# Two-layer hybrid decoder: the spatial-gating constants prepared during branch C's value projection, and the final norm's last squares summed on TensorE

## The chip, the cores and the metric

The kernel runs on one core of a Trainium2 chip. The time is that of one execution on the device in microseconds (us); lower is better. PE is TensorE's matmul row in the profile, PEld its weight loads, DVE is VectorE, ACT ScalarE, POOL GpSimd, SP SyncE; PEq, ACTq and SPq are the queues of these engines, from which DMAs are issued.

## The reference

Two layers on x of 512 tokens by 1024 channels, all float32, then a final RMSNorm. For each layer:

```
h = rmsnorm(x);  proj = h @ w_in
A: differential attention      C: mixture of dilated window attentions
B: vb = layernorm(gelu(..)) in chunks of 128 tokens
   mixed = einsum('gts,bnsgc->bntgc', sgu_w * tril, vb) + sgu_b
   yb = u * mixed * silu(bz)
merged = sum over branches of sigmoid(gate) * (y_branch @ w_branch)
x = x + merged @ w_out
```

What the change touches is B's `mixed`, whose constants are the masked `sgu_w` and a bias, and the final `rmsnorm`, which needs the sum of the squares of 1024 channels for each token.

## The kernel before

Channels lie on the partitions, in eight blocks of 128 (KC = 8), tokens along the free axis. Every large product is made of three float32r matmuls (L408 to L411): a weight tile is split into a rounded part `whi` (ACT, L170) and a remainder `wlo` (DVE, every fifth on POOL, L171). The weights come from HBM in tiles `raw` of 512 KB through SP's queue (L151). Two such tiles have buffers, so a load starts when the tile two places earlier has been split. Six split slots lie ahead of TensorE. Some units ("S") are Strassen products: their operands are first combined by POOL and DVE (L192 to L195), and seven products of 256 columns (`seven`, L503) are added on DVE and POOL (L528) through the tiles `ea`, `eb` and `zs`.

The order of a layer is the list in `plan()`: B's and A's value projections, C's value projection ("val C", during which `mix` on ACT and DVE prepares the Strassen operands of h), attention A with projections as filling, attention C with projections as filling, then the first gate group, `("sgu",)`, the other gate groups between the branch projections `pb`, and the output projection `out`. Within this program order a scheduler places the instructions of each engine by their readiness and priority. At run time each engine runs its own instructions strictly in order.

`i_sgu` (L657) runs right after attention C. On ACT's queue it issues the load of the bias row, broadcast to all partitions, and of the 128x512 weights (L661, L662). `behind_weights` orders these behind the newest weight split. POOL masks the weights (L666). TensorE sums their columns with a matmul by ones (L671) into `ps_s`, of which there is one buffer. DVE makes `add` of that, the bias and a layernorm parameter in four instructions (L675). Then come, for each of four groups, four matmuls (L685), two DVE instructions (L690, L695), and a split into `yB` (L414, L415). `add` lies in a buffer of the tag "t1", which `seven` uses for `eb`.

In the last layer the output blocks 4 to 7 are made in two halves of 256 tokens, LT and RT. For each block `square` (L278) takes squares on ACT (L284) and adds them to `ss` on POOL (LT) or DVE (RT), L288; block 7's stay apart. `final` (L824) has TensorE sum `ss` and block 7's squares over the channels (L386, a matmul for each tile and 128 tokens, each in two passes), DVE scales (L391), POOL takes the power -0.5 (L393), DVE and TensorE spread the result (L400, L405), and eight DVE multiplications and stores follow (L829, L830).

Of the kernel before, what the change touches and what calls it, by code (L numbers as in the profile page):

```python
# [10 lines left out]
F32 = mybir.dt.float32  # L11
# [4 lines left out]
ALU = mybir.AluOpType  # L16
# [3 lines left out]
P = 128  # L20
D = 1024
# [79 lines left out]
def hybrid_kernel(ctx: ExitStack, tc, xT, posr, wpack, tabs, cvec, pvec, rvec, lamv, sguw, outT):  # L101
# [149 lines left out]
    class X:  # L251


        def __init__(self, first=False):
            self.first = first
            self.h = att.tile([P, KC, S], F32R, tag="vs", name="xuh")
            self.l = []
            self.f = []
            self.ss = t2k("ob", name="ssum")

        def raw(self, kc):
            if kc % 2 == 0:
# [15 lines left out]
        def square(self, kc, c=slice(0, S), part=False):  # L278
            xf = self.f[kc // 2][:, kc % 2, c]
            if kc == 0:  # L280
                A.activation(out=self.ss[:, c], in_=xf, func=AF.Square)
            else:
                sq = t2k("t1", name="sq")
                A.activation(out=sq[:, c], in_=xf, func=AF.Square)  # L284
                if part and kc == KC - 1:
                    self.sq = sq
                    return
                (V if kc == KC - 1 or self.first or c.start else G).tensor_tensor(out=self.ss[:, c], in0=self.ss[:, c], in1=sq[:, c], op=ALU.add)  # L288

# [90 lines left out]
    def rms_sum(sqs):  # L380

        n = sqs[0].shape[-1] // P
        ps = ps_s()[:, 0, :]
        for b in range(n):
            for i, sq in enumerate(sqs):
                T.matmul(  # L386
                    ps[:, b : b + 1], lhsT=sq[:, b * P : (b + 1) * P], rhs=ones[:, 0:1], start=i == 0,
                    stop=i == len(sqs) - 1,
                )
        ro = sm.tile([P, 4], F32, tag="ro", name="ro")[:, :n]  # L390
        V.tensor_scalar(out=ro, in0=ps[:, :n], scalar1=1.0 / D, scalar2=EPS, op0=ALU.mult, op1=ALU.add)  # L391
        rp = sm.tile([P, 4], F32, tag="rp", bufs=2, name="rp")[:, :n]
        G.tensor_tensor(out=rp, in0=ro, in1=mhalf[:, :n], op=ALU.pow)  # L393
        return rp
# [153 lines left out]
    def layer(l, xu, parts):  # L548
# [47 lines left out]
        def mix(kc):  # L596
            with behind_weights():
                if kc == 0:
                    split_x(KC - 1)
                    norm["mix"] = mixes(xu.f)  # L600
                next(norm["mix"])
                if kc == KC - 1:
                    next(norm["mix"])
                    if l == 0:
                        lambdas()

        def pair(it, use, bank=ps_pj):

# [47 lines left out]

        def i_sgu():  # L657
            vb, uz = sgu["vb"], sgu["uz"]
            sgw = [att.tile([P, S], F32, tag="kl", bufs=2, name="sgw") for _ in range(2)]
            with behind_weights():  # L660
                nc.scalar.dma_start(out=sgw[0], in_=rvec[l : l + 1, :].partition_broadcast(P))  # L661
                nc.scalar.dma_start(out=sgw[1], in_=sguw[l])  # L662
            t = att.tile([P, 2, 4, S], F32R, tag="vs", name="yB")
            yhl[BR_B] = [[t[:, 0, 0:2], t[:, 0, 2:4]], [t[:, 1, 0:2], t[:, 1, 2:4]]]
            wc = sgw[1].rearrange("p (g t) -> p g t", g=4)
            G.affine_select(  # L666
                out=wc, in_=wc, pattern=[[0, 4], [1, P]], base=0, channel_multiplier=-1, compare_op=ALU.is_ge,
                fill=0.0,
            )
            pw = ps_s()[:, 0, :]  # L670
            T.matmul(pw, lhsT=ones, rhs=sgw[1], start=True, stop=True)  # L671
            add = t2k("t1", name="add")
            for g in range(4):
                gs = slice(g * P, (g + 1) * P)
                V.scalar_tensor_tensor(  # L675
                    out=add[:, gs], in0=pw[:, gs], scalar=ln[:, l, 1, g : g + 1], in1=sgw[0][:, gs], op0=ALU.mult,
                    op1=ALU.add,
                )
            yield 0.9
            for g in range(4):  # L680
                if g % 2 == 0:
                    pms = ps_s()
# [1 line left out]
                for tb in range(4):  # L684
                    T.matmul(  # L685
                        pm[:, tb * P : (tb + 1) * P], lhsT=vb[:, tb, g * P : (g + 1) * P],
                        rhs=wc[:, g, :], start=True, stop=True,
                    )
                ob = t2k("ob")
                V.scalar_tensor_tensor(  # L690
# [6 lines left out]
                )  # L697
                split(yhl[BR_B][0][g // 2][:, g % 2, :], yhl[BR_B][1][g // 2][:, g % 2, :], ob)
                yield 0.9

        def i_val(br):
            if br == BR_A:
# [12 lines left out]
            for tb in range(4):  # L715
# [4 lines left out]
                    out=o[:, :, 64:128], in0=p8, scalar=r, in1=o[:, :, 0:64].bitcast(F32), op0=ALU.mult,  # L720
                    op1=ALU.subtract,
                )

        def i_pp(br, i):
            def use(n, ps, own):
# [97 lines left out]

        def final(c):  # L824
            x_ = xn[0]
            bc = rms_spread(rms_sum([x_.ss[:, c], x_.sq[:, c]]))
            for e in range(KC):
                xf = x_.f[e // 2][:, e % 2, c]
                V.scalar_tensor_tensor(out=xf, in0=xf, scalar=fg[:, e : e + 1], in1=bc, op0=ALU.mult, op1=ALU.mult)  # L829
                (nc.sync, nc.scalar)[e % 2].dma_start(out=outT[e, :, c], in_=xf)  # L830
# [317 lines left out]
```

## Time and profile before

| what | us |
|---|---|
| median of 3 runs | 1116.62 (1115.82 to 1116.85) |
| the profiled execution | 1117.34 |
| its span, first to last instruction | 1115.6 |
| PE busy | 1087.3 (97%) |
| DVE busy | 823.6 (74%) |
| ACT busy | 598.9 (54%) |
| POOL busy | 471.4 (42%) |

Shares are averages over the whole span. Where PE is idle in a stretch, the wait that ended last there tells what it stood for; idle time of the other engines costs nothing by itself.

### The profile page before, as it was taken

Reading aid. Unit: us, or ns where it says so; the run is one execution under the profiler, and the core shown is the slowest. Engines: PE = TensorE matmul, PEld = TensorE weight load, DVE = VectorE, ACT = ScalarE, POOL = GpSimd, SP = SyncE. Lnnn points to the kernel's source line nnn. Section 1 sums busy time; section 2 is a strip of 40 time slices with the busy share of each in tenths; the row PEclk is TensorE's granted clock in tenths of the full one; section 3 lists DMA queues with packets and bytes.
Section 4 is the critical chain, followed back from the end, with each engine's and each line's share of the span. In section 5 each row is a group of like instructions: output and inputs, shape, how many; then the busy total and the mean of one; then the engine's idle time right before and its main releaser. Section 6 shows DMA issues by size and latency. Waiting matters only on the chain.

```text
span 1115.6 us, 17803 instructions
## 1 busy us (share of the span) xinstructions
PE 1087.3 (97%) x6444; PEld 939.6 (84%) x6444; DVE 823.6 (74%) x1519; ACT 598.9 (54%) x1281; POOL 471.4 (42%) x419
## 2 busy tenths in 40 slices
PE   8999999999999999999999999999999999999996
PEld 6787878878778999998888888887888889999886
DVE  6678869877969877774436779787788877787544
ACT  6554747486774444453435456565778534444430
POOL 4004443434534676644211343534342536667420
PEclk9999999999999999999999999999999999999998
DMA  5431313220312233244523313122111313333433
GB/s 194 135 103 58 95 58 96 95 76 1 114 58 87 87 112 102 92 148 152 188 83 103 98 38 114 57 76 76 58 58 57 112 59 101 107 97 103 142 110 99
DMA packets 35064, 105.97 MB, mean 95 GB/s; under 512 B 4704, under 2 KB 7776, under 8 KB 34976
## 3 DMA queue, kind: packets, MB, share of 16 engines
q1 hardware_dynamic: 29936, 98.50, 27.6%
q10 hardware_dynamic: 5040, 6.34, 1.8%
q8 instruction: 51, 0.84, 0.3%
q14 instruction: 37, 0.30, 0.1%
HBM read 100.58 MB, written 4.24 MB: 94 GB/s over the span
## 4 chain that ended last, share of the span: by engine, by line
PE 85%; DVE 5%; DMA 3%; issue 2%; ACT 2%; POOL 1%; POOLq 0%; DVEq 0%; SPq 0%; ACTq 0%
PE ps_pj L409 15%; PE ps_pj L411 14%; PE ps_pj L410 14%; PE ps_to L409 8%; PE ps_to L411 8%; PE ps_to L410 8%; PE ps_s L858 3%; DMA raw<-in_wpack 2%; PE ps_to L898 2%; PE ps_to L434 2%; PE ps_to L436 2%; PE ps_to L435 2%; DVE wlo L171 1%; PE ps_to L929 1%; PE ps_to L1004 1%
## 5 line engine op out<-in xcount | busy, mean ns | idle before, releaser
L170 ACT ACTIVATE whi<-raw 128x512 fp32r<-128x512 f32 x316 | 195.0, 627 | 246.3 <-DMA raw<-in_wpack 74.2
L171 DVE TENSOR_TENSOR wlo<-raw,whi 128x512 fp32r<-128x512 f32 x261 | 223.0, 862 | 99.2 <-ACT whi L170 91.1
L409 PE MATMUL ps_pj<-xh,whi 128*128 128x512 f32 (+1 forms) x544 | 207.9, 382 | 1.0 <-DVE z L462 1.0
L411 PE MATMUL ps_pj<-xh,wlo 128*128 128x512 f32 (+1 forms) x544 | 204.5, 376 | 0.0
L410 PE MATMUL ps_pj<-xl,whi 128*128 128x512 f32 (+1 forms) x544 | 204.0, 375 | 0.0
L171 POOL TENSOR_TENSOR wlo<-raw,whi 128x512 fp32r<-128x512 f32 x55 | 78.8, 1433 | 169.6 <-ACT whi L170 158.2
L409 PEld LDWEIGHTS ps_pj<-xh,whi 128*128 128x128 f32 x544 | 102.6, 189 | 20.0 <-issue 1.6
L411 PEld LDWEIGHTS ps_pj<-xh,wlo 128*128 128x128 f32 x544 | 102.5, 188 | 18.2 <-issue 0.9
L410 PEld LDWEIGHTS ps_pj<-xl,whi 128*128 128x128 f32 x544 | 102.7, 189 | 17.6 <-issue 1.8
L452 POOL TENSOR_TENSOR rsh<-rsh,sinr 128x512 f32<-128x512 f32 x32 | 42.3, 1322 | 132.8 <-DVE rsh L450 121.3
L171 DVE TENSOR_TENSOR wlo<-t,whi 128x512 fp32r<-128x512 f32 x88 | 81.2, 940 | 16.2 <-ACT whi L170 16.0
L411 PE MATMUL ps_to<-mh,wlo 128*128 128x256 f32 x320 | 90.5, 284 | 0.5 <-DVE wlo L171 0.4
L409 PE MATMUL ps_to<-mh,whi 128*128 128x256 f32 x320 | 90.8, 284 | 0.2 <-ACT ea L531 0.2
L410 PE MATMUL ps_to<-ml,whi 128*128 128x256 f32 x320 | 90.4, 283 | 0.0
L874 ACT ACTIVATE pr<-pr,nm 128x128 f32<-128x128 f32 (+3 forms) x128 | 70.6, 553 | 36.4 <-DVE nm L870 36.1
L170 ACT ACTIVATE whi<-t 128x512 fp32r<-128x512 f32 x112 | 65.8, 624 | 42.0 <-DVE t L193 23.4
L409 PE MATMUL ps_to<-xh,whi 128*128 128x256 f32 x240 | 68.5, 285 | 2.6 <-DVE zs L528 2.5
L411 PE MATMUL ps_to<-xh,wlo 128*128 128x256 f32 x240 | 68.4, 286 | 0.7 <-DVE wlo L171 0.7
L410 PE MATMUL ps_to<-xl,whi 128*128 128x256 f32 x240 | 68.2, 284 | 0.0
L870 DVE CUSTOM_DVE_ANT_0 pr<-ps_s,tab 128x128 f32<-128x128 f32 (+3 forms) x128 | 56.2, 483 | 11.8 <-PE ps_s L858 8.3
L409 PEld LDWEIGHTS ps_to<-mh,whi 128*128 128x128 f32 x320 | 61.4, 192 | 1.0 <-ACT ea L531 0.4
L411 PEld LDWEIGHTS ps_to<-mh,wlo 128*128 128x128 f32 x320 | 61.3, 192 | 1.2 <-DVE wlo L171 0.9
(238 smaller groups left out, 2844.9 us busy)
## 6 DMA issues: line engine op xcount, KB each, us to landing
raw<-in_wpack SPq DMA_DIRECT2D x174, 512.0 KB
xf<-in_xT SPq DMA_DIRECT2D x8, 256.0 KB
xr<-in_xT ACTq DMA_DIRECT2D x8, 256.0 KB
x1d<-xf SPq DMA_DIRECT2D x8, 256.0 KB
raw<-in_wpack SPq DMA_DIRECT2D x4, 256.0 KB
xr<-x1d ACTq DMA_DIRECT2D x4, 256.0 KB
xr<-x1d ACTq DMA_DIRECT2D x8, 128.0 KB
out<-xf SPq DMA_DIRECT2D x8, 128.0 KB
```

What stands on the lines that cost most here:

```text
L170: newest[0] = A.activation(out=hi, in_=src, func=AF.Copy).ins
L171: r = (G if on_g else V).tensor_tensor(out=lo, in0=src, in1=hi.bitcast(F32), op=ALU.subtract)
L409: T.matmul(ps, lhsT=wh, rhs=mh, start=first, stop=False)
L410: T.matmul(ps, lhsT=wh, rhs=ml, start=False, stop=False)
L411: T.matmul(ps, lhsT=wl, rhs=mh, start=False, stop=last)
L434: T.matmul(banks[tb], lhsT=mh_[:, ts], rhs=wh, start=kc == 0, stop=False)
L435: T.matmul(banks[tb], lhsT=ml_[:, ts], rhs=wh, start=False, stop=False)
L436: T.matmul(banks[tb], lhsT=mh_[:, ts], rhs=wl, start=False, stop=kc == KC - 1)
L452: G.tensor_tensor(out=sh, in0=sh, in1=sinr, op=ALU.mult)
L858: T.matmul(pss[:, m, at[i]], lhsT=q[HALF[m], a, qs], rhs=k[HALF[m], b, :W], start=t == 0, stop=t == 2,)
L870: V.tensor_tensor_reduce(out=o, in0=pss[:, m, at[i]], in1=tab[:, 0 if br == BR_A else 1, S - W :], op0=ALU.add, op1=ALU.min, scale=-0.125, ...
L874: A.activation(out=o, in_=o, func=AF.Exp, scale=-1.0, bias=nm[:, m : m + 1], accum_out=den[:, m : m + 1],)
```

## The change

The loads of the gating constants and the mask on POOL move into `gating()`, which is called in val C at its third block (kc = 2). The column sum on TensorE and the four DVE instructions move into `gating_add()`, called at the end of val C; they write over the bias tile and no longer take a "t1" buffer. `i_sgu` keeps its four groups only. In the final norm, block 6's squares are no longer added to `ss`: TensorE sums three tiles. For the halves it takes `ss` first for both 128-token groups, then block 6, then block 7, into two banks, and DVE's scaling is done for each group.

```diff
@@ square
-                if part and kc == KC - 1:
-                    self.sq = sq
+                if part and kc >= KC - 2:
+                    self.sq[kc] = sq
                     return
@@ rms_sum
-        ps = ps_s()[:, 0, :]
-        for b in range(n):
-            for i, sq in enumerate(sqs):
-                T.matmul(
-                    ps[:, b : b + 1], lhsT=sq[:, b * P : (b + 1) * P], rhs=ones[:, 0:1], start=i == 0,
-                    stop=i == len(sqs) - 1,
-                )
+        ps2 = ps_s()
+        todo = [(b, i) for b in range(n) for i in range(len(sqs))]
+        if n == 2:
+            todo.sort(key=lambda t: t[1])
+        sums = [ps2[:, b % 2 if n == 2 else 0, b : b + 1] for b in range(n)]
+        for b, i in todo:
+            T.matmul(
+                sums[b], lhsT=sqs[i][:, b * P : (b + 1) * P], rhs=ones[:, 0:1], start=i == 0, stop=i == len(sqs) - 1
+            )
...
-        V.tensor_scalar(out=ro, in0=ps[:, :n], scalar1=1.0 / D, scalar2=EPS, op0=ALU.mult, op1=ALU.add)
+        for o, p in [(ro, ps2[:, 0, :n])] if n == 4 else [(ro[:, b : b + 1], sums[b]) for b in range(n)]:
+            V.tensor_scalar(out=o, in0=p, scalar1=1.0 / D, scalar2=EPS, op0=ALU.mult, op1=ALU.add)
@@ mix
+                if kc == 2:
+                    gating()
@@ i_sgu
-            sgw = [att.tile([P, S], F32, tag="kl", bufs=2, name="sgw") for _ in range(2)]
-            with behind_weights():
-                nc.scalar.dma_start(out=sgw[0], in_=rvec[l : l + 1, :].partition_broadcast(P))
-                nc.scalar.dma_start(out=sgw[1], in_=sguw[l])
...
-            G.affine_select(
...
-            pw = ps_s()[:, 0, :]
-            T.matmul(pw, lhsT=ones, rhs=sgw[1], start=True, stop=True)
-            add = t2k("t1", name="add")
-            for g in range(4):
-                gs = slice(g * P, (g + 1) * P)
-                V.scalar_tensor_tensor(
-                    out=add[:, gs], in0=pw[:, gs], scalar=ln[:, l, 1, g : g + 1], in1=sgw[0][:, gs], op0=ALU.mult,
-                    op1=ALU.add,
-                )
-            yield 0.9
+            add, wc = sgu["w"]
@@ new
+        def gating():
+
+            sgu["w"] = add, wc = [att.tile([P, S], F32, tag="kl", bufs=2, name="sgw") for _ in range(2)]
+            with behind_weights():
+                nc.scalar.dma_start(out=add, in_=rvec[l : l + 1, :].partition_broadcast(P))
+                nc.scalar.dma_start(out=wc, in_=sguw[l])
+            w4 = wc.rearrange("p (g t) -> p g t", g=4)
+            G.affine_select(
+                out=w4, in_=w4, pattern=[[0, 4], [1, P]], base=0, channel_multiplier=-1, compare_op=ALU.is_ge,
+                fill=0.0,
+            )
+
+        def gating_add():
+            add, wc = sgu["w"]
+            pw = ps_s()[:, 0, :]
+            T.matmul(pw, lhsT=ones, rhs=wc, start=True, stop=True)
+            for g in range(4):
+                gs = slice(g * P, (g + 1) * P)
+                V.scalar_tensor_tensor(
+                    out=add[:, gs], in0=pw[:, gs], scalar=ln[:, l, 1, g : g + 1], in1=add[:, gs], op0=ALU.mult,
+                    op1=ALU.add,
+                )
@@ final
-            bc = rms_spread(rms_sum([x_.ss[:, c], x_.sq[:, c]]))
+            bc = rms_spread(rms_sum([x_.ss[:, c], x_.sq[KC - 2][:, c], x_.sq[KC - 1][:, c]]))
```

The first place is DVE's queue at the end of attention C in layer 0. Before (`y` are the splits of A's output, `ob` at L1013 the joining of C's two halves, `ea` and `eb` the sums of a Strassen product):

```order
L415 TENSOR_TENSOR ptl<-ps_to,pth 128x4x128 x2
L415 TENSOR_TENSOR y<-yf,y 128x512 x2
L528 TENSOR_TENSOR ea<-ps_pj,ea 128x256
L1013 TENSOR_TENSOR ob<-ps_to,ob 64x512
L171 TENSOR_TENSOR wlo<-t_3399,whi 128x512
L171 TENSOR_TENSOR wlo<-t_3398,whi 128x512
L171 TENSOR_TENSOR wlo<-t_3399,whi 128x512
L1013 TENSOR_TENSOR ob<-ps_to,ob 64x512
L415 TENSOR_TENSOR y<-yf,y 128x512
L171 TENSOR_TENSOR wlo<-raw,whi 128x512
L1014 SCALAR_TENSOR_TENSOR yf<-ob,zs 128x512
L675 SCALAR_TENSOR_TENSOR add<-ps_s,pv,sgw 128x128 x4
```

The same place with the change, where the lines of the file have moved by 4 to 12 (L678 is the former L690, L683 the former L695):

```order
L419 TENSOR_TENSOR ptl<-ps_to,pth 128x4x128 x2
L532 TENSOR_TENSOR ea<-ps_pj,ea 128x256
L171 TENSOR_TENSOR wlo<-t_3410,whi 128x512
L171 TENSOR_TENSOR wlo<-t_3409,whi 128x512
L678 SCALAR_TENSOR_TENSOR ob<-ps_s,pv,sgw 128x512
L171 TENSOR_TENSOR wlo<-t_3410,whi 128x512
L419 TENSOR_TENSOR y<-yf,y 128x512 x2
L683 SCALAR_TENSOR_TENSOR ob<-ob,uz 128x512
L1025 TENSOR_TENSOR ob<-ps_to,ob 64x512
L532 TENSOR_TENSOR eb<-ps_pj,ea 128x256
L419 TENSOR_TENSOR y<-yf,y 128x512
L1025 TENSOR_TENSOR ob<-ps_to,ob 64x512
```

The four `add` instructions are gone from here, the first gating group stands ahead of the splits of `y`, and so do `ea` and the weight splits.

The second place is DVE's queue at the end of val C in layer 0, with the change (`vs` are C's values, `ml` and `tm` the Strassen operands):

```order
L500 TENSOR_TENSOR tm<-xf,tm 128x512
L368 TENSOR_SCALAR sg<-pv 128x1 x2
L707 SCALAR_TENSOR_TENSOR sgw<-ps_s,pv,sgw 128x128 x2
L419 TENSOR_TENSOR ml<-tm,mh 128x512
L707 SCALAR_TENSOR_TENSOR sgw<-ps_s,pv,sgw 128x128 x2
L730 SCALAR_TENSOR_TENSOR vs<-ps_to,rp,vs 128x8x64 x2
```

The four instructions of L707 are new in this place; what stands around them is as before, except that it comes after them.

The third place is the end of TensorE's queue. Before, and then with the change:

```order
L411 MATMUL ps_to<-mgh,xl 128x256
L386 MATMUL ps_s<-ones,ssum 128x1
L386 MATMUL ps_s<-ones,sq 128x1
L386 MATMUL ps_s<-ones,ssum 128x1
L386 MATMUL ps_s<-ones,sq 128x1
L405 MATMUL ps_s<-dg,ones 128x256
```

```order
L414 MATMUL ps_to<-mgl,xh 128x256
L415 MATMUL ps_to<-mgh,xl 128x256
L390 MATMUL ps_s<-ones,ssum 128x1 x2
L390 MATMUL ps_s<-ones,sq 128x1 x4
L409 MATMUL ps_s<-dg,ones 128x256
```

Two matmuls more, and only the last two of them read block 7's squares. The same six stand, for LT, in one piece ahead of the second RT block; the four of before stood around that block's first three matmuls.

## Rows read from the trace of the kernel before

**Rows 1.** The page's first part: busy time, share of the span, instructions

```profile
PE 1087.3 (97%) x6444; PEld 939.6 (84%) x6444; DVE 823.6 (74%) x1519; ACT 598.9 (54%) x1281; POOL 471.4 (42%) x419
```

**Rows 2.** Windows: length, busy time of each engine, PE clock, DMA share, GB/s

```profile
325.00:365.00 40.00, 36.02 (x247) 31.64 (x246) 38.31 (x56) 20.94 (x38) 21.26 (x16) 1.00 0.38 118
870.00:915.00 45.00, 40.07 (x272) 36.15 (x271) 38.51 (x60) 23.48 (x43) 19.32 (x15) 0.96 0.34 106
0.00:8.00 8.00, 2.84 (x7) 2.27 (x8) 3.10 (x10) 5.02 (x9) 1.63 (x8) 1.00 0.71 229
1104.90:1115.63 10.73, 2.27 (x11) 1.47 (x10) 4.57 (x12) 0.42 (x1) 0.70 (x1) 0.65 0.36 121
```

**Rows 3.** Waits of PE, 320 to 365 us: waiter, releaser, total us, times, longest

```profile
PE ps_s L685 <- DVE add L675: 1.3, 1, 1.3
PE ps_pj L409 <- DVE ea L528: 0.7, 1, 0.7
...
PE ps_s L671 <- POOL sgw L666: 0.5, 1, 0.5
```

**Rows 4.** Waits of PE, 865 to 915 us

```profile
PE ps_to L409 <- DVE zs L528: 2.5, 1, 2.5
PE ps_pj L411 <- DVE wlo L171: 1.5, 1, 1.5
```

**Rows 5.** The tile sgw: line, operation, count, duration ns min/median/max

```profile
L675 DVE SCALAR_TENSOR_TENSOR add<-ps_s,pv,sgw x8: 332/339/344, 335.6 to 882.5; 128x128 f32<-128x128 f32 x8
...
L671 PE MATMUL ps_s<-sgw,ones x4: 591/592/697, 333.5 to 880.3; 128*128 128x512 f32 x4
...
L666 POOL TENSOR_SCALAR_AFFINE_SELECT sgw<-sgw x2: 641/823/1005, 332.4 to 878.7; 128x512 f32<-128x512 f32 x2
```

**Rows 6.** Timeline of DVE in layer 0: start us, us, line, operation

```profile
326.34 2.39 DVE L415 TENSOR_TENSOR y<-yf,y 128x512 fp32r<-128x512 f32 x2 [0.42 <-ACT y L414]
...
335.56 1.11 DVE L675 SCALAR_TENSOR_TENSOR add<-ps_s,pv,sgw 128x128 f32<-128x128 f32 x4
```

**Rows 7.** The chain that ended last, layer 1 (start us, us, what); ACT's queue

```profile
872.94 5.00 DMA raw<-in_wpack
...
880.63 3.42 DMA raw<-in_wpack
...
872.95 0.35 ACTq L661 DMA_DIRECT2D sgw<-in_rvec  x1
```

**Rows 8.** Timelines of DVE, then PE, layer 1, around 905 us

```profile
904.12 1.31 DVE L171 TENSOR_TENSOR wlo<-raw,whi 128x512 fp32r<-128x512 f32 x1
905.36 0.41 DVE L528 TENSOR_TENSOR zs<-ps_to,eb 128x256 f32<-128x256 f32 x1
...
905.91 0.36 PE L409 MATMUL ps_to<-xh,whi 128*128 128x256 f32 x1 [2.54 <-DVE zs L528]
```

**Rows 9.** Windows around 906 us, columns as in rows 2

```profile
906.00:908.00 2.00, 2.00 (x13) 2.00 (x14) 1.06 (x2) 1.82 (x4) 0.37 (x1) 0.71 0.70 207
908.00:910.00 2.00, 2.00 (x6) 1.52 (x5) 0.88 (x2) 1.19 (x2) 0.91 (x1) 0.50 0.28 76
```

**Rows 10.** Val C, layer 0: window, DVE's split of k, first scores

```profile
64.00:68.00 4.00, 4.00 (x20) 3.30 (x19) 2.35 (x5) 1.83 (x4) 0.00 (x0) 1.00 0.21 51
...
91.87 1.56 DVE L415 TENSOR_TENSOR k<-t,k 128x512 fp32r<-128x512 f32 x1
...
95.95 0.96 PE L858 MATMUL ps_s<-k,q 64*128 64x128 f32 x12
```

**Rows 11.** The end: ACT's last squares, PE's sums, DVE's scaling

```profile
1105.48 0.42 ACT L284 ACTIVATE sq<-xf 128x256 f32<-128x256 f32 x1 [0.59 <-DVE xf L813]
...
1105.78 0.38 PE L386 MATMUL ps_s<-ones,ssum 128*128 128x1 f32 x2 [0.85 <-DVE ssum L288]
...
1106.47 0.36 PE L386 MATMUL ps_s<-ones,sq 128*128 128x1 f32 x2
...
1106.87 0.16 DVE L391 TENSOR_SCALAR ro<-ps_s 128x2 f32<-128x2 f32 x1 [1.14 <-PE ps_s L386]
```

More of the change, by code (lines that the diff above doesn't have):

```diff
@@ L259, in __init__ @@
             self.ss = t2k("ob", name="ssum")
+            self.sq = {}
         def raw(self, kc):
@@ L658, in i_sgu @@
             vb, uz = sgu["vb"], sgu["uz"]
-            sgw = [att.tile([P, S], F32, tag="kl", bufs=2, name="sgw") for _ in range(2)]
-            with behind_weights():
-                nc.scalar.dma_start(out=sgw[0], in_=rvec[l : l + 1, :].partition_broadcast(P))
-                nc.scalar.dma_start(out=sgw[1], in_=sguw[l])
             t = att.tile([P, 2, 4, S], F32R, tag="vs", name="yB")
             yhl[BR_B] = [[t[:, 0, 0:2], t[:, 0, 2:4]], [t[:, 1, 0:2], t[:, 1, 2:4]]]
-            wc = sgw[1].rearrange("p (g t) -> p g t", g=4)
-            G.affine_select(
-                out=wc, in_=wc, pattern=[[0, 4], [1, P]], base=0, channel_multiplier=-1, compare_op=ALU.is_ge,
-                fill=0.0,
-            )
-            pw = ps_s()[:, 0, :]
-            T.matmul(pw, lhsT=ones, rhs=sgw[1], start=True, stop=True)
-            add = t2k("t1", name="add")
-            for g in range(4):
-                gs = slice(g * P, (g + 1) * P)
-                V.scalar_tensor_tensor(
-                    out=add[:, gs], in0=pw[:, gs], scalar=ln[:, l, 1, g : g + 1], in1=sgw[0][:, gs], op0=ALU.mult,
-                    op1=ALU.add,
-                )
-            yield 0.9
+            add, wc = sgu["w"]
             for g in range(4):
@@ L686, in i_sgu @@
                         pm[:, tb * P : (tb + 1) * P], lhsT=vb[:, tb, g * P : (g + 1) * P],
-                        rhs=wc[:, g, :], start=True, stop=True,
+                        rhs=wc[:, g * P : (g + 1) * P], start=True, stop=True,
                     )
@@ L722, in i_val @@
                 )
+            gating_add()
         def i_pp(br, i):
```

## The prediction

> **What bounds the kernel now.** I read the page's first part first: TensorE is busy 1087.3 us, 97% of the span, and DVE 74% [rows 1]. The kernel is bound by TensorE, so an edit pays only if it shortens TensorE's work, fills its idle time, or raises its clock. The idle time is 1115.6 - 1087.3 = 28.3 us, and the windows tell where it lies [rows 2]: 5.2 us in the first 8 us, 8.5 us in the last 10.7, and then 40.00 - 36.02 = 4.0 us in the 40 us where attention C of layer 0 ends, and 45.00 - 40.07 = 4.9 us in the corresponding 45 us of layer 1. These two stretches are where the gating units run, and in the first of them DVE is busy 38.31 of 40 us: DVE, not TensorE, sets the pace there.
>
> The waits of TensorE say for what it stood. In layer 0 it waited 1.3 us for `add` (the first gating matmul needs the only `ps_s` buffer, which DVE's four `add` instructions are still reading), 0.5 us for POOL's mask, and 0.7 us for `ea` [rows 3]. In layer 1 the two long ones are 2.5 us for `zs` and 1.5 us for a weight remainder `wlo` [rows 4]. The chain of layer 1 shows a weight load of 5.00 us where a later one took 3.42; the broadcast load of the bias had been put on ACT's queue 0.01 us after it [rows 7]. The gap of 2.5 us also costs afterwards: the granted clock was 0.71 and then 0.50 of full speed, the latter being the lower of TensorE's two levels (1.2 of 2.4 GHz), in the two windows that follow [rows 9], which is 2 x 0.29 + 2 x 0.50 = 1.6 us of lost work. After the longest gap of layer 0, 1.3 us, the window's clock was still 1.00 [rows 2, 3].
>
> **The change part by part.** *Gating, layer 0.* The mask and the column sum have left the end of attention C, so the waits of 1.3 and 0.5 us have nothing left to stand on: -1.8 us. The wait for `ea` arose because `ea` stood behind two splits of `y` that together took 2.39 us [rows 6]; in the new order it stands ahead of them, so I take its 0.7 us too. Sum: -2.5 us. It could be 0 at the least, if other DVE work ends just as late, since DVE is full; it can't be over the 4.0 us of idle time. DVE's own relief is 1.1 us for the four `add` instructions [rows 6]; it is the means by which these waits go and is not counted again.
>
> *Gating, layer 1.* The two loads of 256 KB no longer run beside the weight load, which I expect to fall from 5.00 to about 3.4 us, 1.6 us sooner; that covers the wait of 1.5 us for `wlo`: -1.5 us. The gap of 2.5 us ends when DVE reaches `zs`, behind a weight remainder of 1.31 us [rows 8]. DVE gets there 1.1 us sooner without `add` [rows 6]: -1.1 us, and 1.4 us of the gap stay. If so the gap is about as long as layer 0's, after which the clock did not fall; as it would lie just above, I take half of the 1.6 us of lost clock: -0.8 us. Sum: -3.4 us. The ends are 0 and 4.9 + 1.6 = 6.5 us.
>
> *Gating, its new place.* Each layer's column sum is two passes of 0.59 us on TensorE, the same as before [rows 5]: moved, not added. In val C TensorE is never idle and POOL does nothing for long stretches (0.00 of 4 us) [rows 10], so POOL's mask of 0.64 to 1.00 us [rows 5], and its wait for the load, delay nobody in layer 0; in layer 1 POOL has a few weight splits there, six slots ahead of their use. On ACT's queue the two issues stand between weight splits with the same reserve. On DVE the four instructions (4 x 0.34 = 1.4 us at most [rows 5]) come ahead of `ml`, `vs` and the first rotary step, and all of these come later by that. Who waits is the first scores of attention A: the split of k ended at 91.87 + 1.56 = 93.43 us and TensorE reached the scores at 95.95 [rows 10]. The reserve is 2.5 us, and TensorE itself gets there about 1 us later, as it now has the column sum before it. I cost the move at 0, with +0.4 us a layer as the upper end if DVE also waits a us for TensorE's sum.
>
> About loads, the row shows 5.00 us beside the two gating loads against 3.42 without [rows 7]. The DMA engines' share in val C is 0.21 in the window shown [rows 10], so a load that takes 1.6 us more still lands before its slot is due, and the sum has 0 for it. The Trainium skill ("DMA: Bandwidth & Descriptors", section "Issuing engines are not separate DMA queues") says that DMAs from ACT and SP run on the same 16 engines and interleave, so that another issuing queue buys no bandwidth; the row of 5.00 us agrees. By that rule alone the 1.6 us would come back in val C of each layer, and the sum would be 3.2 us worse; that is a rival below.
>
> *Final norm.* For LT, TensorE now sums three tiles instead of two: two matmuls more, at the pitch of the four of before, (1106.47 - 1105.78) / 3 = 0.23 us [rows 11], in a stretch where TensorE is the pace: +0.46 us. For RT, TensorE takes `ss` and block 6 while ACT still makes block 7's squares (1105.48 to 1105.90), and only two matmuls are left behind these, where before the last of the four started at 1106.47 [rows 11]. The first can start at about 1106.0, the last 0.23 us later, so DVE's scaling begins some 0.2 us earlier than 1106.87: -0.2 us. The second scaling instruction for each half is covered by the matmul between them. Net: +0.2 us, between -0.2 (the LT matmuls hidden) and +0.5.
>
> **Sum.** -2.5 - 3.4 + 0.2 = -5.7 us. The profiled execution took 1117.34 us, which gives 1111.6. It stands 0.72 us above the median of the runs (1116.62), so I forecast **1110.9 us** for the median.
>
> **The rivals.**
>
> *Absorbed (no change).* DVE is full at the end of attention C [rows 2]. Its first gating group now stands ahead of the splits of `y`, C's last joining and some weight splits, so other work may come late in place of what goes, and in layer 1 the late load may simply repeat. Then only the direct waits of layer 0 go: -1.8 + 0.2 = -1.6 us, 1115.0 us. For it: a full engine hands its lateness on. Against it: in both layers 1.1 us of DVE work and one wait on POOL leave the stretch, and nothing enters.
>
> *Slower: a second late load.* The gap of 2.5 us in layer 1 came from a late `raw` tile, and the clock fell after it [rows 8, 9]; layer 0, with nearly the same order, had no such gap. The new order changes when DVE's weight splits free the buffers, and so when loads start. If such a gap opens in layer 0 as well, it costs 2.5 + 1.6 = 4.1 us there. With layer 1 as it was and only the direct waits gone, that is +4.1 - 1.8 + 0.2 = +2.5 us: 1119.1 us. The point from which it decides is a gap over the 1.3 us that left the clock at 1.00, so that the lower clock is paid too.
>
> *Loads in val C.* The gating loads push weight loads back by 5.00 - 3.42 = 1.6 us in each layer and the slots run dry: -5.7 + 3.2 = -2.5 us, 1114.1 us. It is the rule on DMA queues above. Against it speaks the window in val C: DMA share 0.21, TensorE without idle time [rows 10].
>
> *The change doesn't do what it says.* The new queues show the four instructions, and the two matmuls that alone read block 7, in their new places, so I give this no chance of its own.
>
> **How the numbers follow.** Forecast 0.61; absorbed 0.21; slower 0.12; loads in val C 0.06. The forecast's own range is 1107.5 to 1114: gains from 3 to 9 us, where the ends of the terms together would allow 10. A measurement of this kernel tells some 0.2%, 2.2 us, from no change, so "same" is 1114.4 to 1118.9. The forecast and the loads lie below that (0.67), absorbed inside (0.21), the second late load above (0.12). The range that should hold 8 in 10 takes in the forecast's range, the loads and the absorbed case, with 2 us around the latter: 1107.5 to 1117. What is left out is the slower case and the largest gains.
>
> **What would show it.** In the profile after: PE's waits for `add` and for the mask are gone; the windows of the two stretches hold under 2 and under 3 us of idle time; the first weight load at the end of attention C in layer 1 takes about 3.4 us; the clock doesn't reach 0.50 around 906 us; val C has no idle TensorE and the first scores come within 1.5 us of 95.95; six sums stand in a row at the end, with about 0.2 us less between block 7's squares and DVE's scaling. The prediction is wrong if the idle time of the two stretches together stays over 6 us, if a gap of over 2 us with a lower clock appears elsewhere, or if TensorE stands still in val C.

## The result and the profile after

The changed kernel takes **1110.15 us**, the median of 4 runs (1109.49 to 1110.97); the kernel before, run on the same chip, 1116.73 us (4 runs, 1115.82 to 1118.82). The ratio is 0.9939, 95% interval [0.9922, 0.9956]: 6.6 us faster. The forecast was 1110.9 us, range 1107.5 to 1117.0, with 0.67 on faster. The profiled executions differ a little more: spans of 1115.6 and 1108.1 us, so 7.5 us.

The first part of the changed kernel's page, which answers to [rows 1]:

```profile
PE 1083.9 (98%) x6452; PEld 938.5 (85%) x6452; DVE 818.9 (74%) x1520; ACT 598.9 (54%) x1281; POOL 473.2 (43%) x418
```

TensorE's idle time fell from 28.3 to 1108.1 - 1083.9 = 24.2 us. The windows of the changed kernel (length, busy time of PE, PEld, DVE, ACT and POOL, PE clock, DMA share, GB/s) answer to [rows 2] and [rows 9]:

```profile
325.00:365.00 40.00, 36.31 (x252) 33.16 (x251) 35.99 (x53) 21.20 (x40) 18.53 (x15) 1.00 0.31 94
870.00:915.00 45.00, 42.39 (x303) 39.27 (x302) 41.46 (x62) 24.51 (x44) 25.05 (x18) 1.00 0.33 100
906.00:908.00 2.00, 2.00 (x11) 1.65 (x10) 2.00 (x2) 0.94 (x2) 1.55 (x1) 1.00 0.80 254
908.00:910.00 2.00, 2.00 (x15) 1.84 (x14) 2.00 (x5) 0.85 (x2) 0.62 (x1) 1.00 0.67 190
```

In layer 1 TensorE's idle time fell from 4.93 to 2.61 us and the clock is 1.00 throughout. In layer 0 it fell only from 3.98 to 3.69 us. Together 6.30 us remain, and one of the prediction's signs of being wrong was over 6 us. TensorE's waits in the changed kernel, 315 to 365 us and then 860 to 960 us (waiter, releaser, total us, times, longest), answer to [rows 3] and [rows 4]:

```profile
PE ps_to L415 <- DVE wlo L171: 2.3, 2, 1.5
PE ps_pj L413 <- ACT yB L418: 0.9, 1, 0.9
PE ps_s L673 <- DVE ob L678: 0.5, 1, 0.5
...
PE ps_to L415 <- POOL wlo L171: 1.4, 1, 1.4
PE ps_s L673 <- DVE ob L678: 0.9, 1, 0.9
PE ps_pj L413 <- DVE zs L532: 0.3, 1, 0.3
```

The waits for `add`, for the mask and for `ea` are gone, and the wait of 2.5 us for `zs` is 0.3 us. Others stand in their places: two weight remainders in layer 0 (2.3 us), one of POOL's in layer 1 (1.4 us), and `ob`, the result of a gating group.

The moved work is found in the tile `sgw` (line, engine, operation, count, duration ns min/median/max, first and last start us), as in [rows 5]:

```profile
L707 DVE SCALAR_TENSOR_TENSOR sgw<-ps_s,pv,sgw x8: 341/343/347, 77.3 to 621.6; 128x128 f32<-128x128 f32 x8
...
L704 PE MATMUL ps_s<-sgw,ones x4: 590/592/594, 75.3 to 618.8; 128*128 128x512 f32 x4
...
L696 POOL TENSOR_SCALAR_AFFINE_SELECT sgw<-sgw x2: 692/748/804, 66.8 to 609.8; 128x512 f32<-128x512 f32 x2
```

All of it now runs in val C, at its old durations. With its constants ready, the first gating group itself starts much earlier too: its matmuls begin at 319.2 us instead of 336.8 in layer 0, and at 863.5 instead of 884.4 us in layer 1. The split of k in val C, from the timeline of DVE (start us, us), answers to [rows 10]:

```profile
92.73 1.55 DVE L419 TENSOR_TENSOR k<-t,k 128x512 fp32r<-128x512 f32 x1
```

It ends at 94.28 us instead of 93.43, and the first scores of attention A start at 96.7 us instead of 95.95: TensorE still comes later than k.

To see where the time went, I split the span at two points that both kernels have: the first block `xf` at the end of each layer, from the row of DVE's `xf`. Before, it was written at 521.5 us in layer 0 and 1070.4 us in layer 1; after, at 519.5 and 1062.8 us.

| | before | after | difference |
|---|---|---|---|
| start to first `xf` of layer 0 | 521.5 | 519.5 | -2.0 |
| from there to first `xf` of layer 1 | 548.9 | 543.3 | -5.6 |
| from there to the end of the span | 45.2 | 45.3 | +0.1 |

"Layer 0" and "layer 1" below mean these two pieces, as differences to the profiled execution of the kernel before. Each is read from one execution of either program. Four programs with the changed gating in layer 1 and nothing added (the changed kernel, gating_only, lt_two_tiles, layer1_only) agree there within 0.1 us, -5.5 to -5.6; in layer 0 they spread from -1.0 to -2.0 where the gating was changed.

### The profile page after: what moved, and what is told of

Same layout as the page of the kernel before. It is cut to its first block, busy times and chain, and to the rows that moved or that the text cites. A ratio compares the mean times of both kernels' runs of the same rounds, so it can differ in the third digit from the quotient of the medians.

```text
span 1108.1 us, 17821 instructions
## 1 busy us (share of the span) xinstructions
PE 1083.9 (98%) x6452; PEld 938.5 (85%) x6452; DVE 818.9 (74%) x1520; ACT 598.9 (54%) x1281; POOL 473.2 (43%) x418
## 4 chain that ended last, share of the span: by engine, by line
PE 87%; DVE 6%; issue 2%; DMA 2%; ACT 2%; POOL 1%; SPq 0%; POOLq 0%; DVEq 0%; ACTq 0%
PE ps_pj L413 15%; PE ps_pj L415 15%; PE ps_pj L414 14%; PE ps_to L415 8%; PE ps_to L414 8%; PE ps_to L413 8%; PE ps_s L870 3%; PE ps_to L910 2%; PE ps_to L438 2%; PE ps_to L440 2%; PE ps_to L439 2%; PE ps_to L941 1%; DVE wlo L171 1%; PE ps_to L1016 1%; DMA raw<-in_wpack 1%
```

## The experiments

### Which part: the gating move, the final norm, or both

*gating_only* is the changed kernel with the final norm as before; *norm_only* is the kernel before with the changed final norm. The hunks on the squares, `rms_sum` and `final` stand in norm_only and not in gating_only, for instance:

```diff
-            bc = rms_spread(rms_sum([x_.ss[:, c], x_.sq[KC - 2][:, c], x_.sq[KC - 1][:, c]]))
+            bc = rms_spread(rms_sum([x_.ss[:, c], x_.sq[:, c]]))
```

> The gating part of the change alone, with the final norm as before. My account: the gain is all in the two stretches at the end of attention C, and the final norm costs 0.2 us, so this is 6.8 us faster than before (about 1109.9 us against 1116.7), no slower than the whole change. Rival, that the final norm gives a good part of it: less than 5 us faster.

> The final norm's part alone, with the gating as before. My account: two more matmuls at 0.23 us for LT and 0.2 us less at the end, so +0.2 us, not to be told from no change (1116.5 to 1117.3). Rival: 1 us or more faster.

gating_only: 1109.85 us (1109.17 to 1110.49), ratio 0.9934 [0.9922, 0.9946]. norm_only: 1116.73 us, ratio 0.9997 [0.9988, 1.0006]. The whole gain is the gating move's.

*lt_two_tiles* keeps three tiles for the second half of the final norm only:

```diff
-                if part and kc >= KC - 2:
+                if part and kc >= (KC - 2 if c.start else KC - 1):
```

> The changed kernel with the final norm's first half (LT) summed from two tiles as before, and the second half (RT) from three. The prediction's terms: the two extra matmuls of LT (0.46 us) go and the 0.2 us of RT stay, so 1109.7, not told apart from 1110.15 by the comparison but by the end of the trace, where TensorE's sums of LT take about 0.5 us less. Rival: the LT sums lie beside other work, no change in the trace's end either.

1109.54 us (1109.36 to 1110.0), ratio 0.9931 [0.9918, 0.9943]: the fastest median of the study, and not told apart from the changed kernel. The timelines of TensorE show the difference. First the changed kernel, LT's sums and the next matmul, then RT's sums (start us, us, operation, idle time before it), answering to [rows 11]:

```profile
1087.21 0.50 PE L390 MATMUL ps_s<-ones,ssum 128*128 128x1 f32 x4
1087.57 1.03 PE L390 MATMUL ps_s<-ones,sq 128*128 128x1 f32 x8
1088.46 0.36 PE L413 MATMUL ps_to<-mg,xh 128*128 128x256 f32 x1
...
1097.60 0.50 PE L390 MATMUL ps_s<-ones,ssum 128*128 128x1 f32 x4
1097.96 0.58 PE L390 MATMUL ps_s<-ones,sq 128*128 128x1 f32 x4
1098.79 0.61 PE L390 MATMUL ps_s<-ones,sq 128*128 128x1 f32 x4 [0.24 <-ACT sq L285]
```

And lt_two_tiles, LT's sums:

```profile
1087.68 0.50 PE L390 MATMUL ps_s<-ones,ssum 128*128 128x1 f32 x4
1088.04 0.36 PE L413 MATMUL ps_to<-mg,xh 128*128 128x256 f32 x1
1088.24 0.50 PE L390 MATMUL ps_s<-ones,sq 128*128 128x1 f32 x4
1088.61 0.36 PE L414 MATMUL ps_to<-mg,xh 128*128 128x256 f32 x1
```

With three tiles LT's sums hold TensorE for 1088.46 - 1087.21 = 1.25 us, with two for 0.36 + 0.37 = 0.73 us: 0.52 us, where 0.46 was expected. For RT, ACT's last squares of the changed kernel start at 1098.32 and take 0.42 us, and DVE's scaling ends at 1099.59:

```profile
1099.21 0.38 DVE L395 TENSOR_SCALAR ro<-ps_s 128x1 f32<-128x1 f32 x2 [0.98 <-PE ps_s L390]
```

That is 1099.59 - 1098.74 = 0.85 us from the squares to the scaled sum, against 1107.03 - 1105.90 = 1.13 us before [rows 11]: 0.28 us saved.

### Which layer

*layer0_only* and *layer1_only* make the gating move in one layer and leave the final norm as before. In the other layer `i_sgu` calls both new functions itself, so everything stands in its old place there, but `add` is written over the bias tile and takes no "t1" buffer:

```diff
-                if kc == 2:
+                if kc == 2 and l == 0:
                     gating()
...
+            if l != 0:
+                gating()
+                gating_add()
+                yield 0.9
...
-            gating_add()
+            if l == 0:
+                gating_add()
```

> The gating part in layer 0 alone, final norm as before. The prediction's terms: 2.5 us faster than before (about 1114.3). By the two traces, in which layer 0 lost some 2 us and layer 1 the rest: 2 us faster. Rival, that the gain is the clock and the late gap of layer 1 alone: within 1 us of before.

> The gating part in layer 1 alone, the final norm as before. layer0_only gave -2.8 us and gating_only -7.1, so if the layers add up: -4.3 us, about 1112.4, ratio 0.9962. By the prediction's own terms (-3.4 for layer 1): 1113.4. If layer 1 carries nearly all (the idle time and the lower clock, 4.9 + 1.6 us): 1110.5.

layer0_only: 1113.82 us (1113.08 to 1115.27), ratio 0.9976 [0.9966, 0.9985]. layer1_only: 1111.53 us (1111.53 to 1111.82), ratio 0.9949 [0.9935, 0.9962]. In time these are -2.7 and -5.7 us (0.0024 and 0.0051 of 1116.7), together 8.4, more than the 6.6 to 7.4 us of both; for layer1_only none of the three expected times was met (1111.5 us lies between them). The pieces of the span tell why the sum is too large. In layer1_only, layer 0 is +0.1 and layer 1 -5.5. In layer0_only, layer 0 is -1.8, but layer 1, in which only the buffer of `add` was changed, is -1.5 as well. There the gap before `zs` and the drop of the clock are missing. The windows of layer0_only:

```profile
870.00:915.00 45.00, 40.67 (x277) 36.13 (x276) 39.17 (x59) 22.69 (x42) 22.78 (x17) 1.00 0.32 106
905.00:910.00 5.00, 4.14 (x18) 2.81 (x17) 5.00 (x7) 2.50 (x5) 1.72 (x2) 1.00 0.61 210
```

and its longest waits of TensorE, 860 to 946 us:

```profile
PE ps_pj L411 <- DVE wlo L171: 1.5, 1, 1.5
PE ps_to L411 <- DVE wlo L171: 1.4, 2, 1.0
```

The 1.5 us for `wlo` of [rows 4] is still there, the 2.5 us for `zs` is not, and the clock is 1.00 where it was 0.96 [rows 2]. So the gap of 2.54 us with its slow clock [rows 8, 9] can go while layer 1's loads, mask, sum and `add` stay in their old places. The next experiment makes the same edit to the buffer, in both layers.

*add_in_place* is the kernel before, with `add` written over the bias tile:

```diff
-            add = t2k("t1", name="add")
+            add = sgw[0]
```

> Before, with the sum written over the bias tile, so that it takes no t1 buffer; all else as before. My account, in which this buffer plays no part: within 1 us of before. Rival, that the buffer held back the Strassen sums (eb): 2 us or more faster.

1116.0 us, ratio 0.9991 [0.9982, 1.0]; layer 0 is 0.0, layer 1 -1.6. Its waits of TensorE, 860 to 935 us, again lack `zs`, and the clock from 905 to 910 us is 1.00:

```profile
PE ps_to L411 <- DVE wlo L171: 1.6, 2, 1.2
PE ps_pj L411 <- DVE wlo L171: 1.5, 1, 1.5
```

DVE does the same work here as in the kernel before, in another order. Its timelines show what the gap stood on, first in the kernel before, then in add_in_place:

```profile
901.78 1.76 DVE L193 TENSOR_TENSOR t<-t,raw 128x512 f32<-128x512 f32 x1 [2.19 <-POOL t L192]
...
900.08 0.41 DVE L528 TENSOR_TENSOR zs<-ps_to,eb 128x256 f32<-128x256 f32 x1
```

Before, DVE stood idle for 2.19 us until POOL delivered an operand `t` (POOL itself had waited for a weight tile), and `zs` (905.36 us [rows 8]) came behind `t` in DVE's queue; with `add` in place, `zs` stands ahead of it. In these two programs, which share the edit to the buffer, layer 1 is 1.5 to 1.6 us shorter, in one execution each; add_in_place's median is 0.9 us below the kernel before, with an interval that reaches no change. So some 4 of layer 1's 5.6 us come from elsewhere. Whether the buffer acts by itself or only by the order that the scheduler then makes was not separated.

Nor did the slow clock vanish from add_in_place: it stands in layer 0, where the kernel before had 1.00 from 325 to 365 us, and layer 0 is 0.0 even so:

```profile
330.00:335.00 5.00, 4.99 (x24) 4.51 (x25) 4.94 (x7) 2.30 (x4) 2.89 (x3) 0.66 0.50 193
```

### Which cause: the loads, POOL's wait, or DVE's time

*loads_and_mask_early* moves the loads and the mask only; column sum and `add` stay in `i_sgu`, with the "t1" buffer, and the final norm is as before.

```diff
             t = att.tile([P, 2, 4, S], F32R, tag="vs", name="yB")
             yhl[BR_B] = [[t[:, 0, 0:2], t[:, 0, 2:4]], [t[:, 1, 0:2], t[:, 1, 2:4]]]
-            add, wc = sgu["w"]
+            add = gating_add()
+            _, wc = sgu["w"]
+            yield 0.9
```

> The loads and the mask stand in val C, but the column sum and DVE's four instructions stay after attention C and take their t1 buffer as before. My account of the loads (layer 1: a weight load of 5.0 us becomes 3.4, 1.5 us; the waits on the mask, 0.5 us; and with an earlier load perhaps the late gap and its clock): 2 to 4 us faster than before. Rival, that DVE's relief of 1.1 us a stretch does it all: within 1 us of before.

1109.81 us (1108.84 to 1110.68), ratio 0.9933 [0.9921, 0.9946]: the whole gain, more than either account allowed, and with the "t1" buffer kept. But it does not test the loads alone, because the scheduler places by readiness. With its data there, `add` no longer runs at 335.56 us [rows 6]. DVE's timeline, and the windows around it:

```profile
320.52 1.13 DVE L706 SCALAR_TENSOR_TENSOR add<-ps_s,pv,sgw 128x128 f32<-128x128 f32 x4 [2.84 <-PE ps_s L703]
...
320.00:325.00 5.00, 5.00 (x43) 4.76 (x42) 3.18 (x8) 1.78 (x4) 1.65 (x3) 1.00 0.01 3
...
330.00:335.00 5.00, 4.34 (x37) 4.15 (x35) 5.00 (x9) 4.16 (x9) 1.27 (x2) 1.00 0.42 154
```

`add` now runs at 320.52 us, where DVE is busy 3.18 of 5 us and had been idle for 2.84 us; from 330 to 335 us DVE is busy without a break.

This program also holds the control that the prediction lacked when it compared weight loads of 5.00 and 3.42 us [rows 7]. At 329 us no gating load is in flight, only the weight load that was issued 1.25 us earlier (327.78 us), and yet the chain has:

```profile
329.03 5.37 DMA raw<-in_wpack
```

In the kernel before a second weight load, issued at 874.20 us, ran beside the one of 5.00 us too.

*adds_late* is the same kernel with the sum and `add` tied behind the newest weight splits, so that `add` comes late again while its data come early:

```diff
             pw = ps_s()[:, 0, :]
-            T.matmul(pw, lhsT=ones, rhs=wc, start=True, stop=True)
-            for g in range(4):
...
+            with behind_weights():
+                T.matmul(pw, lhsT=ones, rhs=wc, start=True, stop=True)
+                for g in range(4):
...
```

> As loads_and_mask_early (loads and mask in val C, sum and add in the gating unit), except that the column sum and the four add instructions are tied behind the newest weight splits, as the loads of the kernel before were. In the built order the column sum stays early on TensorE, but add stands nine DVE rows later, next to the gating groups, and the first gating group, which needs the ps_s buffer that add reads, follows about 90 TensorE rows later than in loads_and_mask_early. Theory (what counts is DVE's 1.4 us of add a layer, and the gating group behind it, in DVE's full stretch): most of the gain goes, 1112.5 to 1116. Rival (what counts is that the loads and the mask on POOL's queue are early): the gain stays, 1109.5 to 1110.5.

1113.48 us (1112.61 to 1114.76), ratio 0.9966 [0.9953, 0.9978], 3.7 us above loads_and_mask_early. Both theories are half right: with early data and a late `add`, half of the gain stays. But `add` is not all that moved: the first gating group, which needs the buffer that `add` reads, moved with it. The gating matmuls of layer 0 in the kernel before, the changed kernel, loads_and_mask_early and adds_late (start of the first and the last in us):

```profile
L685 PE MATMUL ps_s<-sgw,vb x32: 271/275/348, 336.8 to 354.0; 128*128 128x128 f32 x32
L673 PE MATMUL ps_s<-sgw,vb x32: 272/275/377, 319.2 to 346.4; 128*128 128x128 f32 x32
L671 PE MATMUL ps_s<-sgw,vb x32: 270/275/275, 323.8 to 347.1; 128*128 128x128 f32 x32
L671 PE MATMUL ps_s<-sgw,vb x32: 272/275/307, 334.1 to 352.2; 128*128 128x128 f32 x32
```

The tile `add` in layer 0 of adds_late:

```profile
L707 DVE SCALAR_TENSOR_TENSOR add<-ps_s,pv,sgw x4: 331/332/335, 332.1 to 332.9; 128x128 f32<-128x128 f32 x4
```

and TensorE's waits there, 315 to 365 us:

```profile
PE ps_to L411 <- DVE wlo L171: 0.8, 1, 0.8
PE ps_pj L409 <- ACT yB L414: 0.8, 2, 0.6
PE ps_pj L409 <- DVE ea L528: 0.7, 1, 0.7
PE ps_pj L409 <- DVE eb L528: 0.6, 1, 0.6
PE ps_pj L411 <- DVE wlo L171: 0.6, 1, 0.6
```

TensorE waits for neither `add` nor the mask any more, and still layer 0 is +0.2: the waits that remain are for five other results, four of them DVE's. In loads_and_mask_early layer 0 is -2.4.

*dve_work_late* approaches it from the other side: the changed kernel, with four DVE instructions of `add`'s size put back into the gating unit. Nothing reads them.

```diff
             add, wc = sgu["w"]
+            dum = att.tile([P, P], F32, tag="dum", bufs=1, name="dum")
+            for g in range(4):
+                gs = slice(g * P, (g + 1) * P)
+                V.scalar_tensor_tensor(
+                    out=dum, in0=ny[BR_C][:, 3, gs], scalar=ln[:, l, 1, g : g + 1], in1=add[:, gs], op0=ALU.mult,
+                    op1=ALU.add,
+                )
```

> The changed kernel with four DVE instructions of the size of those that left (128 columns each, two SBUF operands, result unread) in the gating unit. By the prediction's term for DVE's relief (1.1 us in each stretch, which in layer 1 shortens the late gap and keeps the clock up): 2 us or more slower than the changed kernel. By what the run with early loads alone showed: within 1 us.

1113.22 us (1112.93 to 1113.49), ratio 0.9967 [0.9955, 0.998]: 3.1 us more than the changed kernel, as expected by the prediction's term for DVE's relief (2 us or more). The tile `dum`, then the window and the longest wait of TensorE in layer 1:

```profile
L671 DVE SCALAR_TENSOR_TENSOR dum<-yf,pv,sgw x8: 339/343/1377, 340.4 to 895.2; 128x128 f32<-128x128 f32 x8
...
870.00:915.00 45.00, 40.97 (x274) 37.36 (x274) 39.47 (x60) 23.10 (x43) 23.16 (x16) 0.96 0.30 94
...
PE ps_s L680 <- DVE ob L685: 2.2, 1, 2.2
```

A gap of over 2 us and a clock of 0.96 are back, in another place: one `dum` of 1.35 us (890.03 us) stands right ahead of this `ob`. In either layer one of the four instructions takes about 1.4 us instead of 0.34, so that the eight hold DVE for 4.8 us, not for 2.7. They also stand later than `add` did (first at 340.4 us, against 335.6), among the gating groups.

*copies_late* puts the transfers back: the changed kernel, with two copies of 256 KB from HBM to HBM on ACT's queue where the loads had been.

```diff
+            dum = dr.tile([2, P, S], F32, name="dum")
+            with behind_weights():
+                nc.scalar.dma_start(out=dum[0], in_=rvec[l : l + 1, :].partition_broadcast(P))
+                nc.scalar.dma_start(out=dum[1], in_=sguw[l])
             add, wc = sgu["w"]
```

> The changed kernel with two DMAs of 256 KB (HBM to HBM, so that nobody waits for them) put on ACT's queue where the gating loads were. If the loads' share of the DMA engines was what cost (weight loads of 5.0 instead of 3.4 us), 1.5 to 4 us slower than the changed kernel (1111.7 to 1114); the chain shows a longer weight load there. Rival, that only the work that waited for the loads cost: within 1 us of the changed kernel.

1110.25 us (1108.36 to 1110.66), ratio 0.9937 [0.9923, 0.995]: 0.1 us above the changed kernel, where the interval leaves some 1.5 us either way. Yet the chain that ended last has a weight load longer than any of [rows 7]:

```profile
328.07 6.48 DMA raw<-in_wpack
...
336.59 3.48 DMA raw<-in_wpack
```

*pool_waits_late* puts back a wait on POOL's queue: a load of 64 KB where the loads had been, and a mask of 128 columns that waits for it; nothing reads it.

```diff
+            dum = att.tile([P, P], F32, tag="dum", bufs=1, name="dum")
+            with behind_weights():
+                nc.scalar.dma_start(out=dum, in_=sguw[l, :, 0:P])
+            G.affine_select(
+                out=dum, in_=dum, pattern=[[1, P]], base=0, channel_multiplier=-1, compare_op=ALU.is_ge, fill=0.0,
+            )
             add, wc = sgu["w"]
```

> The changed kernel with a small load (64 KB) where the gating loads were, and a mask on POOL of 128 columns that waits for it and whose result nobody reads. If POOL, held by the mask's wait, was what cost (its next weight split and operand sums stand behind it), 1 to 3 us slower than the changed kernel. Rival, that POOL's wait is covered: within 1 us.

1111.28 us (1110.87 to 1112.18), ratio 0.995 [0.9937, 0.9964]: 1.1 us more than the changed kernel, between the two accounts; the intervals do not separate it from the changed kernel. POOL stood 3.8 us for the two loads:

```profile
POOL dum L670: 3.8, 2
```

*all_three_late* puts one copy, POOL's wait and DVE's work back together, ahead of dve_work_late's four instructions:

```diff
+            with behind_weights():
+                nc.scalar.dma_start(out=cp[0], in_=rvec[l : l + 1, :].partition_broadcast(P))
+                nc.scalar.dma_start(out=dum2, in_=sguw[l, :, 0:P])
+            G.affine_select(
+                out=dum2, in_=dum2, pattern=[[1, P]], base=0, channel_multiplier=-1, compare_op=ALU.is_ge, fill=0.0,
+            )
```

> The changed kernel with all three additions at once where the kernel before had its work: a copy of 256 KB and the load of 64 KB on ACT's queue, POOL's mask of 128 columns that waits for this load, and the four DVE instructions of 128 columns; nothing reads them. If the prices found alone add up (0 + 1.1 + 3.1): 1114.4 us, ratio 0.9978, so that some 2.3 us of the gain lie elsewhere (the buffer ps_s and the sum ahead of the gating matmuls). If they hit the same wait and hide each other: 1113.2. If they make each other worse, up to the time of the kernel before: 1116.7.

1112.61 us (1111.68 to 1114.11), ratio 0.9961 [0.9947, 0.9975]. The prices do not add up: with all three it is no slower than with DVE's work alone, nearest to the case in which they hide each other. Only some 2.5 of the 6.6 us come back. Nor does the price of DVE's work stay in one layer: dve_work_late, with the same eight instructions, is -1.5 and -2.2 us in layers 0 and 1, this program +0.4 and -4.2.

## Why the prediction was right, and where its steps were not

The forecast time, its sign and its sum (5.7 us; 6.6 measured) came out. That the gain is all in the gating part, and none in the final norm, is shown by gating_only and norm_only. The sum itself is partly luck: two of its terms came out by another way than the one they were worked out by, and one of the prediction's own signs of being wrong came true (6.30 us of idle time left in the two stretches, with 6 as the limit). The idle time of the two stretches gave only 2.6 us, that of the whole span 4.1 of the 7.5 us; the other 3.4 us are a shorter busy time, 1087.3 to 1083.9 us, with 8 matmul instructions more. The prediction had only 0.8 us of clock for that; where the rest comes from was not taken apart.

**Layer 0, -2.5 us: near in size, wrong in form.** Three programs with the same gating part (the changed kernel, lt_two_tiles, gating_only) show -2.0, -1.5 and -1.0. The three waits did go, but the prediction's test, idle time under 2 us in the 40 us, failed: 3.69 us. New waits for weight remainders and for `yB` stand there. adds_late shows that removing named waits is not the gain: they were gone and layer 0 was +0.2. loads_and_mask_early, in which `add` and the first gating group stand 10 to 12 us earlier, is -2.4, so it is one of these two, or both, that paid; no run separates them. (dve_work_late, which puts DVE's work back and leaves the first group early, is -1.5 in layer 0.) Counted from attention C's last scores to the first `acc`, layer 0 went from 84.7 us (312.8 to 397.5) to 81.8 (313.4 to 395.2). 1.2 us of that is the column sum of two passes of 0.59 us, which returns in part as the 0.7 us by which the first scores come later.

**Layer 1, -3.4 us: it was -5.6, the term that was mis-sized.** Its three parts:

- *The slow weight load, -1.5 us: this step failed.* Its reading was not sound, as the 5.00 us had a second weight load beside it as well as the gating loads, and a load took 5.37 us without any gating load (loads_and_mask_early). Nothing that could be measured was paid for the transfers: copies_late is 0.1 us above the changed kernel while a load takes 6.48 us. And a wait of 1.4 us for `wlo` is still there, now POOL's. In the changed kernel no DMA is in the chain of layer 1 from 860 to 915 us at all; in layer 0 a load of 3.50 us is. This bears on the rule that was weighed as a rival (the Trainium skill, "DMA: Bandwidth & Descriptors", section "Issuing engines are not separate DMA queues"): the rows fit it, since a load took 6.48 us beside another weight load and the copies from ACT's queue, against 5.37 us beside a weight load alone, though in one execution each; but the sharing cost the kernel no time that could be measured.
- *DVE's relief, -1.1 us of the 2.5 us gap: right in sign, wrong in mechanism.* The gap is 0.3 us. Ahead of it DVE was not busy with work that `add` delayed: it stood idle for 2.19 us until POOL delivered `t`, and `zs` came behind `t`. POOL had waited for a weight tile, which is what the rival *slower* says of this gap, not this step. add_in_place and layer0_only lose the gap without relieving DVE in layer 1, by the order of the two, so it was a matter of order and not a sum of durations.
- *The clock, half of 1.6 us: the slow clock went, but its price was not borne out.* Gap and clock together were worth 1.5 to 1.6 us in those two programs, less than the 2.5 + 1.6 us that stand in [rows 8, 9]. The single executions tell more of the clock alone. Of layer0_only's ten, six have a mean clock of 0.995, like the kernel before's 0.993 to 0.995, and take 1114.1 us on average; four have 0.997 or 0.998 and take 1113.9 us. By the prediction's way of counting, 0.002 of a span of 1112 us is 2.2 us; the difference is 0.2. copies_late has 0.995 in all five executions, the changed kernel 0.996 to 0.997, and their medians lie 0.1 us apart.

What then makes the other 4 us of layer 1? By dve_work_late it would be mostly DVE's late work, as its layer 1 is -2.2 instead of -5.6; but all_three_late, with the same work put back and more, is -4.2. POOL's wait gave 1.9 us of layer 1 back (-3.7 in pool_waits_late). By adds_late early data with a late `add` give -3.7 there. These prices overlap and cannot be added, and how they share the 4 us is not shown.

**Val C, 0 us: right.** First scores at 96.7 us lie within the 1.5 us allowed, and TensorE is never idle there (busy 35.00 of 35 us from 62 to 97 us, 36.00 of 36 from 604 to 640 us). POOL waited there for its loads, 47.7 us in two waits, and no wait for POOL's mask is left in the trace:

```profile
  POOL sgw L696: 47.7, 2
```

**The final norm, +0.2 us: right, as far as it can be told.** The terms were +0.46 and -0.2, the traces show +0.52 and -0.28; norm_only cannot tell +0.2 from 0.

**The rivals.** *Absorbed* had the mechanism of layer 0's idle time right (new waits take the place of the old) but not the time. *A slower second late load* did not come: layer 0's longest wait is 1.5 us, with the clock at 1.00. *Loads in val C* needed TensorE to stand still there, and it does not.

**Left open.** About half of the gain is accounted for: DVE's work put back costs 3.1 us (dve_work_late), sum and `add` tied late cost 3.7 us (adds_late). Why early data alone keep the other half is not settled. One rival was never tested by itself: the first gating group, which the changed kernel starts 17.6 and 20.9 us earlier, so that its matmuls and its `yB` leave the full stretch; it stays early in dve_work_late and all_three_late. In adds_late it starts at 334.1 and 877.2 us, 3 to 7 us earlier than in the kernel before, so there it may be the chain of load, mask and sum ahead of it. No run took this chain apart, and putting the mask alone late, with its data early, was not tried. The pieces of single executions also scatter: norm_only, with the gating of the kernel before, is +1.4 in layer 0, where its clock is 0.66 from 330 to 335 us.

## What to carry to other kernels

Where an engine other than the bound one is full for a stretch, the waits that the profile names there are not the price of the stretch: take them away, and the next ones in line stand in their place. The time of the work that is moved is not the price either: here 4.8 us of DVE's time put back cost 3.1 us, and moving two times 1.1 to 1.4 us away, together with what hung on it, gave 6.6 us. When a step's data come early, a scheduler that places by readiness moves the step and its followers too, so early data can be worth as much as moving the work. For a long gap, look at what its releaser itself stood behind before you price it: here `zs` waited behind an instruction that was idle for POOL, and a change of order alone took the gap away. And before a slow load is put down to the loads beside it, look for a row in which only the suspects are missing.

## What the runs showed of the hardware

A weight load of 512 KB took 3.4 to 3.5 us when no other load was issued near it, 5.37 us with another weight load issued 1.25 us before it, 5.00 us beside another weight load and the two gating loads [rows 7], and 6.48 us beside another weight load and two copies of 256 KB; the kernel with the longest of them was 0.1 us slower than the changed kernel, which an interval of some 1.5 us does not tell from nothing.

After a gap of 2.54 us TensorE's clock fell to 0.50 of full speed [rows 8, 9], its lower level. The prediction set the length of a single gap as what decides, and that does not hold in these runs: copies_late, whose longest wait of TensorE from 315 to 365 us is 0.7 us, falls to 0.72 (a mean over 5 us) after two windows in which TensorE is busy 3.98 and 4.33 of 5 us, while the changed kernel, with a wait of 1.5 us and 3.45 and 4.09 us in the same two windows, stays at 1.00. The third window in copies_late, then in the changed kernel:

```profile
345.00:350.00 5.00, 4.43 (x18) 3.56 (x18) 5.00 (x7) 2.18 (x5) 2.78 (x2) 0.72 0.49 187
...
345.00:350.00 5.00, 3.76 (x27) 3.38 (x27) 5.00 (x6) 2.69 (x5) 2.83 (x2) 1.00 0.45 170
```

The four DVE instructions take 332 to 344 ns each late in attention C [rows 5] and 341 to 347 ns in val C: the place changed what the kernel pays, not their duration.
